# Up-projections of a ConvFFN trunk: nine of 22 chunks per layer by seven products, in pairs, with more low parts made by accumulating DMA

## The chip, the cores and the metric

The kernel runs on one core of a Trainium2 chip. TensorE (PE in the profile) multiplies matrices out of SBUF into the banks of PSUM; VectorE (DVE), ScalarE (ACT) and GpSimd (POOL) work on elements; SyncE (SP) only issues DMAs here. Each engine has a queue of its own and works through it in order; an instruction that needs another engine's result waits on a semaphore, and everything behind it on its queue waits too. The metric is the device time of one execution in microseconds (us), as the median of several runs. Lower is better.

## The reference

Two layers over a residual stream of 512 tokens by 1024 features, all in float32. Each layer has an attention and then a gated ConvFFN. Only the ConvFFN is touched here, and in it only the up-projection:

```python
def conv_ffn(xn, w_up, cw, cb, w_down):
    a = xn @ w_up                       # 512x1024 by 1024x5632
    ap = jnp.pad(a, ((0, 0), (CONV_W - 1, 0), (0, 0)))
    a = sum(ap[:, j:j + T] * cw[j] for j in range(CONV_W)) + cb    # three taps
    gate, val = jnp.split(a, 2, axis=-1)
    return (jax.nn.gelu(gate, approximate=True) * val) @ w_down
```

w_up has 5632 columns: 2816 gate columns and 2816 value columns. A chunk is 128 gate columns and the 128 value columns that go with them, so there are 22 chunks in a layer.

## The kernel before, in words

**Products in three parts.** TensorE multiplies in a shorter float format (float32r). To keep float32's accuracy each operand is split into a high part (the value cast down) and a low part (the value minus its high part), and each product is made of three: high by high, high by low and low by high (`mm3`, lines 260 to 263).

**Weights.** A piece is a tile of 128 x 1024 raw weights (512 KB): all 1024 rows of the 128 gate columns of a chunk, or of its value columns. The class `Weights` walks through all pieces of the kernel in one order. SP loads them (line 46), two pieces ahead of the split. `high()` casts a piece on ScalarE (line 54). The low part is made in one of two ways:

```python
    def low(self):            # VectorE: raw - high                          (line 66)
        self.nc.vector.tensor_tensor(pair[:, 1], raw, pair[:, 0].bitcast(F32), ALU.subtract)
    def high_added(self):     # ScalarE: pair[:, 1] = -raw, rounded (line 61); then a DMA adds raw (line 81)
        self.high(True)
        self.low_added()      # self.nc.gpsimd.dma_start(pair[:, 1], raw, accum_op=ALU.add)
```

The second way costs VectorE nothing: ScalarE writes a negated, rounded copy, and a DMA that is issued on GpSimd's queue reads the raw piece and adds it to that copy in SBUF. The raw tile can't be used again until that DMA has landed.

**Plain chunk.** Two pieces (gate, value), each in a bank of 128 x 512 of PSUM: 8 blocks of 128 rows of w_up, three products each, 512 tokens wide. That makes 48 matmuls of 512 columns (`up`).

**Seven-product chunk.** The chunk's product is written as a 2 x 2 block product: the weights as a11, a12 (the gate piece's first and second half of the rows of w_up) and a21, a22 (the value piece's), and the activations as four quarters (half of the features by half of the tokens, LO and HI). Strassen's scheme in Winograd's form then needs seven block products and not eight: with the weights A11, A12 and A22 and the sums S1 = a21 + a22, S2 = S1 - a11, S3 = a11 - a21, S4 = a12 - S2. Each block product is 4 blocks of rows by three parts, 12 matmuls of 256 columns, so a chunk has 84 of those (`prod`, `half_mm`). The four quarters of the result, o1 to o4, lie in the halves of two banks. Between the products o1 is copied out as s1 (ScalarE), and VectorE makes s12 = o2 + s1 and s17 = o3 + s1 (lines 926 and 927) and later adds them into o4, o3 and o2 (lines 935 to 941). A12 goes on in o1's place. The sums of the activations (XA, XB) are made once a layer by `sums_in`: two additions on GpSimd (line 646), then VectorE and ScalarE. The weights' sums and splits of a chunk are made by `seven_weights` (lines 665 to 694), a generator that is advanced piece by piece with `next(steps)`: two casts of 1024 for A11|A12 and S3|S2, one for S1|S4, one of 512 for A22, and the low parts all on VectorE (lines 683 to 690).

**Loop of a layer** (`ffn`, from line 602). Chunks 0 and 1 are made before the loop (`first_products`), and the weights of chunks 2 and 3 are split ahead (`W.split`). The loop then goes over c = 2 to 21. While TensorE works on chunk c, the other engines finish chunk c - 1 and prepare chunk c + 2:

- `product()`: VectorE multiplies gate by value of chunk c - 2 into hc (line 629), and GpSimd's queue stores the hc of the chunk before to memory (line 627);
- `taps()`: for the gate and the value bank of chunk c - 1 ScalarE makes the first tap and the bias (line 611), VectorE the other two taps (lines 612 and 614);
- `glu()`: ScalarE's GELU (line 632);
- `weights(c + 2)`: the steps that prepare the weights of chunk c + 2.

Seven-product chunks are 6, 8, ... 18 (seven in a layer), each with a plain chunk behind it. The four first row blocks of that plain chunk's first piece are multiplied inside the seven-product chunk, between A22 and S4 (`begun`), so that TensorE has work while S4 waits. Low parts by DMA are used for chunks 20 and 21 alone (four pieces a layer, `plain_weights`).

From chunk 18 on the layer's down-projection is prepared too: `pair_load` and `down_sums` load and add its weights, `pair_sums` (lines 725 to 728), `pair_highs` (line 735) and `pair_lows` (line 739) split the gated activations, which come back from memory.

**What sets the order.** The kernel runs under `manual_schedule`: each engine's queue holds its instructions in the order in which the program issues them. Tiles come from pools: p8 (16 tiles of two 1024-wide parts: split weights, activations' sums), p4 (10 tiles of 128 x 1024: raw weights, the weights' sums `wsum`, the taps' `bb`), p2 (8 small ones: hc, s1, s12, s17) and 8 banks of PSUM. An instruction that writes a new tile waits until the last reader of the tile's former content is done, and a DMA that reads it is such a reader.

Of the kernel before, what the change touches and what calls it, by code (L numbers as in the profile page):

```python
# [1 line left out]

# [6 lines left out]
F32 = mybir.dt.float32  # L9
F32R = mybir.dt.float32r  # L10
# [5 lines left out]
T = 512  # L16
# [10 lines left out]
SEVEN = range(6, 19, 2)  # L27
# [73 lines left out]
def trunk_kernel(ctx, tc, x, norm_gains, w_qkv_a, w_o_a, w_q_b, w_o_b, kv_norm, w_kvf, b_f,  # L101
# [500 lines left out]
    def ffn(l, bd, cp, nxt, ahead):  # L602
# [58 lines left out]
        halves = {}  # L661
# [6 lines left out]
        def seven_weights(c):  # L668

            r0, r1 = W.take(2)  # L670
            w = [t8([128, 2, 1024], F32R, name="w") for _ in range(4)]
            sa, sb = (t4([128, 1024], name="wsum") for _ in range(2))
            a11, a12, a21, a22 = r0[:, 0:512], r0[:, 512:1024], r1[:, 0:512], r1[:, 512:1024]
            act.copy(w[0][:, 0], r0)
            dve.tensor_tensor(sa[:, 0:512], a11, a21, ALU.subtract)
# [3 lines left out]
            act.copy(w[1][:, 0], sa)  # L679
            dve.tensor_tensor(sb[:, 512:1024], a12, sa[:, 512:1024], ALU.subtract)  # L680
            yield
            dve.tensor_tensor(w[1][:, 1], sa, w[1][:, 0].bitcast(F32), ALU.subtract)
            act.copy(w[2][:, 0], sb)
            yield
            dve.tensor_tensor(w[0][:, 1], r0, w[0][:, 0].bitcast(F32), ALU.subtract)
            act.copy(w[3][:, 0, 0:512], a22)
            yield
            dve.tensor_tensor(w[2][:, 1], sb, w[2][:, 0].bitcast(F32), ALU.subtract)
            yield
            dve.tensor_tensor(w[3][:, 1, 0:512], a22, w[3][:, 0, 0:512].bitcast(F32), ALU.subtract)  # L690
            v = [t.rearrange("p s (q k c) -> p s q k c", q=2, k=4) for t in w]
            halves[c] = dict(A11=v[0][:, :, 0], A12=v[0][:, :, 1], S3=v[1][:, :, 0], S2=v[1][:, :, 1],
                             S1=v[2][:, :, 0], S4=v[2][:, :, 1], A22=v[3][:, :, 0])

        def plain_weights(c):
            for _ in range(2):
                if c < NF - 2:
                    W.high()
                    W.low()
                else:  # L700
                    W.high_added()
                yield

        def weights(c):
            return seven_weights(c) if c in SEVEN else plain_weights(c)

# [191 lines left out]
        extra = sums_in()  # L898
        begun = None
        before = None  # L900
        for c in range(2, NF):
# [5 lines left out]
            steps = weights(c + 2) if c + 2 < NF else iter(())  # L907
            banks = [bank([128, T], name="up") for _ in range(2)]
            if c in SEVEN:
                w = halves.pop(c)  # L910
                W.n_get += 2
                x11, x21, x22 = [(xT[0][i], xT[1][i], s) for i, s in ((0, LO), (1, LO), (1, HI))]
                o1, o2, o3, o4 = banks[0][:, LO], banks[0][:, HI], banks[1][:, LO], banks[1][:, HI]
                s1, s12, s17 = (t2([128, 256], name="csum") for _ in range(3))

                def prod(o, a, x, start=False):
                    half_mm(o, w[a], x[0:2], x[2], start)

                prod(o1, "A11", x11, True)
                prod(o2, "S2", (*XB, HI))  # L920
                prod(o3, "S3", (*XA, HI), True)
                product()
                bb = taps(*before)
                act.copy(s1, o1)
                next(steps)
                dve.tensor_tensor(s12, o2, s1, ALU.add)
                dve.tensor_tensor(s17, o3, s1, ALU.add)
                glu(before[0], bb)
                prod(o1, "A12", x21)
                prod(o2, "S1", (*XA, LO))  # L930
                prod(o3, "A22", (*XB, LO))
                next(steps)
                next(steps, None)
                dve.tensor_tensor(o4, o2, s17, ALU.add)
                begun = W.get(), bank([128, T], name="up")
                up(*begun, range(4))
                prod(o2, "S4", x22)
# [756 lines left out]
```

## Time and profile before

| quantity | value |
|---|---|
| time, median of 3 runs | 1120.49 us (1119.68 to 1120.97) |
| time of the profiled execution | 1119.51 us |
| its span in the profile | 1117.5 us |
| TensorE's granted clock, mean | 0.999 of full speed |
| busy: TensorE | 1108.2 us, 99% |
| busy: VectorE | 891.2 us, 80% |
| busy: ScalarE | 614.0 us, 55% |
| busy: GpSimd | 182.8 us, 16% |
| moved by DMA | 217.34 MB, 194 GB/s in the mean |
| first up-projection of the loop (c = 2), layer 0 | starts at about 204.5 us of the span |
| first product of the down-projection, layer 0 | at about 417 us |

The span runs from the first to the last instruction; the profiled execution's own time is 2.0 us longer. Busy time is the time in which an engine executes, as a share of the span. A row of a view of single instructions gives the start (us from the start of the span), the length, the engine, the line of the source, the operation, output and inputs by the program's names, and the tiles' shapes; the brackets behind it say how long the engine was idle ahead of it and what ended that. Instructions of one engine overlap at their ends, so the distance from one start to the next is the price of an instruction in a full queue, and the length is not.

### The profile page before, as it was taken

Reading aid. Unit: us, or ns where it says so; the run is one execution under the profiler, and the core shown is the slowest. Engines: PE = TensorE matmul, PEld = TensorE weight load, DVE = VectorE, ACT = ScalarE, POOL = GpSimd, SP = SyncE. Lnnn points to the kernel's source line nnn. Section 1 sums busy time; section 2 is a strip of 40 time slices with the busy share of each in tenths; the row PEclk is TensorE's granted clock in tenths of the full one; section 3 lists DMA queues with packets and bytes.
Section 4 is the critical chain, followed back from the end, with each engine's and each line's share of the span. In section 5 each row is a group of like instructions: output and inputs, shape, how many; then the busy total and the mean of one; then the engine's idle time right before and its main releaser. Section 6 shows DMA issues by size and latency. Waiting matters only on the chain. (4 is left out here: it accounts for less than half of the span.)

```text
span 1117.5 us, 17262 instructions
## 1 busy us (share of the span) xinstructions
PE 1108.2 (99%) x6258; PEld 950.8 (85%) x6258; DVE 891.2 (80%) x1456; ACT 614.0 (55%) x1036; POOL 182.8 (16%) x277
## 2 busy tenths in 40 slices
PE   9999999999999999999999999999999999999997
PEld 6988889889899888888878888889889889988886
DVE  6567788888888689997697777848888888589894
ACT  5454575545445456576462688745445445457572
POOL 2832101200000121000001545500300000121000
PEclk9999999999999999999999999999999999999999
DMA  9469854343433699893447666464333444599862
GB/s 325 151 222 408 313 174 134 94 123 105 141 119 116 158 354 368 303 324 110 132 152 272 199 171 164 115 197 130 97 102 116 132 124 122 149 352 374 317 245 75
DMA packets 179183, 217.34 MB, mean 194 GB/s; under 512 B 11225, under 2 KB 131017, under 8 KB 179098
## 3 DMA queue, kind: packets, MB, share of 16 engines
q1 hardware_dynamic: 169594, 183.99, 50.6%
q0 software_dynamic: 9504, 32.25, 9.0%
q8 instruction: 49, 0.80, 0.3%
q14 instruction: 36, 0.29, 0.1%
HBM read 166.08 MB, written 39.63 MB: 184 GB/s over the span
## 5 line engine op out<-in xcount | busy, mean ns | idle before, releaser
L611 ACT ACTIVATE bb<-up,conv 128x512 f32<-128x512 f32 x80 | 60.7, 777 | 149.4 <-DVE up L941 76.2
L66 DVE TENSOR_TENSOR w<-wraw,w 128x1024 fp32r<-128x1024 f32 x98 | 125.0, 1306 | 18.4 <-ACT w L54 14.0
L261 PE MATMUL acc<-w 128*128 128x512 f32 (+1 forms) x311 | 120.6, 388 | 0.3 <-DVE mix L323 0.3
L263 PE MATMUL acc<-w 128*128 128x512 f32 (+1 forms) x311 | 120.4, 387 | 0.0
L54 ACT CAST w<-wraw 128x1024 fp32r<-128x1024 f32 x110 | 111.4, 1046 | 15.0 <-PE v_ps L262 6.9
L261 PE MATMUL up<-xch,w 128*128 128x512 f32 (+1 forms) x292 | 104.9, 359 | 0.0
L261 PE MATMUL up<-xbh,w 128*128 128x512 f32 (+1 forms) x292 | 104.8, 359 | 0.0
L262 PE MATMUL up<-xcl,w 128*128 128x512 f32 (+1 forms) x292 | 104.8, 359 | 0.0
L262 PE MATMUL up<-xbl,w 128*128 128x512 f32 (+1 forms) x292 | 104.8, 359 | 0.0
L263 PE MATMUL up<-xch,w 128*128 128x512 f32 (+1 forms) x292 | 104.7, 358 | 0.0
L263 PE MATMUL up<-xbh,w 128*128 128x512 f32 (+1 forms) x292 | 104.7, 358 | 0.0
L262 PE MATMUL acc<-w 128*128 128x512 f32 (+1 forms) x267 | 103.3, 387 | 0.0
L627 POOL DMA_DIRECT2D hD<-hc x42 | 24.3, 579 | 316.9 <-DVE hc L629 316.5
L261 PEld LDWEIGHTS acc<-w 128*128 128x128 f32 x311 | 58.4, 188 | 12.4 <-DVE mix L323 0.7
L263 PEld LDWEIGHTS acc<-w 128*128 128x128 f32 x311 | 58.4, 188 | 12.0 <-DVE w L739 0.2
L612 DVE SCALAR_TENSOR_TENSOR bb<-up,conv,bb 128x511 f32<-128x511 f32 x80 | 59.5, 744 | 7.8 <-ACT bb L611 7.8
L261 PE MATMUL up<-xsh,w 128*128 128x256 f32 x224 | 63.4, 283 | 0.0
L262 PE MATMUL up<-xsl,w 128*128 128x256 f32 x224 | 63.4, 283 | 0.0
L263 PE MATMUL up<-xsh,w 128*128 128x256 f32 x224 | 63.4, 283 | 0.0
L261 PEld LDWEIGHTS up<-xch,w 128*128 128x128 f32 x292 | 55.1, 189 | 8.3
L614 DVE SCALAR_TENSOR_TENSOR bb<-up,conv,bb 128x510 f32<-128x510 f32 x80 | 59.9, 749 | 2.8
L261 PEld LDWEIGHTS up<-xbh,w 128*128 128x128 f32 x292 | 55.1, 189 | 8.3
(310 smaller groups left out, 3018.1 us busy)
## 6 DMA issues: line engine op xcount, KB each, us to landing
wraw<-in_w_up_dram SPq DMA_DIRECT2D x88, 512.0 KB
dT<-dsums SPq DMA_DIRECT2D x24, 512.0 KB
dsums<-in_w_down_dram SPq DMA_DIRECT2D x22, 512.0 KB
dsums<-in_w_down_dram SPq DMA_DIRECT2D x44, 256.0 KB
hD<-hc POOLq DMA_DIRECT2D x44, 256.0 KB, 4.8
dact<-hD SPq DMA_DIRECT2D x44, 256.0 KB
wraw<-dT SPq DMA_DIRECT2D x22, 512.0 KB
wraw<-in_w_down_dram SPq DMA_DIRECT2D x22, 512.0 KB
```

Source lines behind the costliest of these rows:

```text
L54: self.nc.scalar.copy(pair[:, 0], raw)
L66: self.nc.vector.tensor_tensor(pair[:, 1], raw, pair[:, 0].bitcast(F32), ALU.subtract)
L261: pe.matmul(o, ah, bh, start=first, stop=False, skip_group_check=shared)
L262: pe.matmul(o, ah, bl, start=False, stop=False, skip_group_check=shared)
L263: pe.matmul(o, al, bh, start=False, stop=last, skip_group_check=shared)
L611: act.activation(bb[:, s, :], ps, AF.Identity, bias=cp[:, 3, ch:ch + 1], scale=cp[:, 2, ch:ch + 1])
L612: dve.scalar_tensor_tensor(bb[:, s, 1:], ps[:, :T - 1], cp[:, 1, ch:ch + 1], bb[:, s, 1:], ALU.mult, ALU.add)
L614: dve.scalar_tensor_tensor(bb[:, s, 2:], ps[:, :T - 2], cp[:, 0, ch:ch + 1], bb[:, s, 2:], ALU.mult, ALU.add)
L627: pool.dma_start(hD[c - 1], hc.pop(c - 1))
```

## The change

**More seven-product chunks, in pairs.** SEVEN becomes 6, 8, 9, 11, 12, 14, 15, 17, 18: nine a layer. Chunk 6 stands alone; then come four pairs of neighbours, with a plain chunk behind each pair.

**Low parts.** A table ADDED says which pieces of plain chunks get their low part by an accumulating DMA: the first pieces of chunks 4, 5, 7, 10, 13, 16 and 20 and the second pieces of 4, 5, 20 and 21. The others are subtracted by VectorE: so are both pieces of chunk 19 and, new, the first piece of chunk 21. In the first chunk of each pair, and in chunk 6 (chunks whose predecessor is plain), the three 1024-wide low parts (A11|A12, S3|S2, S1|S4) are made by DMA as well (`add_low`); in the second chunk of a pair VectorE subtracts them (`sub_low`), that of S1|S4 at a later place (`late`). The low part of A22 stays on VectorE throughout. That makes 26 accumulating DMAs a layer, where there were 4.

**Weights in two generators.** `weights_a(c)` runs during chunk c - 2 (A11|A12 and the first sums, or a plain chunk's two pieces), `weights_b(c)` during chunk c - 1 (S1|S4 and A22). The steps that are left at the end of a chunk now stay for the next one, unless the next chunk is plain or the one after it has seven products.

**Order of products.** The first chunk of a pair, and chunk 6, starts with A11; then come `begin()` inside the taps (the copy s1, the product S3, the sum s17, the product S2) and `join()` (s12), then A22, A12 and S1. Before its S4 the first chunk of a pair multiplies A11 and S3 of the second chunk; the second chunk then starts with S2 (`begun`). The second chunk has, ahead of its S4, the first half of the plain chunk's first piece, as every seven-product chunk had before. A22 now stands ahead of A12 and S1.

```diff
-SEVEN = range(6, 19, 2)
+SEVEN = 6, 8, 9, 11, 12, 14, 15, 17, 18
+
+ADDED = (4, 5, 7, 10, 13, 16, 20), (4, 5, 20, 21)
...
+        def add_low(w, raw):
+            act.activation(w[:, 1], raw, AF.Copy, scale=-1.0)
+            pool.dma_start(w[:, 1], raw, accum_op=ALU.add)
+
+        def sub_low(w, raw, n=1024):
+            dve.tensor_tensor(w[:, 1, :n], raw, w[:, 0, :n].bitcast(F32), ALU.subtract)
+
+        def weights_a(c):
+            if c >= NF:
+                return
+            if c not in SEVEN:
+                for i in range(2):
+                    if c in ADDED[i]:
+                        W.high_added()
+                    else:
+                        W.high()
+                        W.low()
+                    yield
+                return
             r0, r1 = W.take(2)
...
             act.copy(w[0][:, 0], r0)
+            if c - 1 not in SEVEN:
+                add_low(w[0], r0)
             dve.tensor_tensor(sa[:, 0:512], a11, a21, ALU.subtract)
             dve.tensor_tensor(sb[:, 0:512], a21, a22, ALU.add)
             yield
             dve.tensor_tensor(sa[:, 512:1024], sb[:, 0:512], a11, ALU.subtract)
-            act.copy(w[1][:, 0], sa)
+            if c - 1 not in SEVEN:
+                act.copy(w[1][:, 0], sa)
+                add_low(w[1], sa)
...
+        def weights_b(c):
+            if c not in SEVEN:
+                return
+            (w0, w1), r0, a12, a22, sa, sb = rest.pop(c)
+            if c - 1 in SEVEN:
+                act.copy(w1[:, 0], sa)
+                sub_low(w0, r0)
...
             dve.tensor_tensor(sb[:, 512:1024], a12, sa[:, 512:1024], ALU.subtract)
+            act.copy(w[1][:, 0, 0:512], a22)
+            if c - 1 in SEVEN:
+                sub_low(w1, sa)
             yield
+            act.copy(w[0][:, 0], sb)
+            if c - 1 in SEVEN:
+                late.append(lambda: sub_low(w[0], sb))
+            else:
+                add_low(w[0], sb)
+            sub_low(w[1], a22, 512)
...
-            steps = weights(c + 2) if c + 2 < NF else iter(())
+            steps = chain(steps, weights_b(c + 1), weights_a(c + 2))
...
+                def begin():
+                    act.copy(s1, o1)
+                    prod(o3, "S3", (*XA, HI), True)
+                    dve.tensor_tensor(s17, o3, s1, ALU.add)
+                    prod(o2, "S2", (*XB, HI))
+
+                def join():
+                    dve.tensor_tensor(s12, o2, s1, ALU.add)
+
+                if begun:
+                    prod(o2, "S2", (*XB, HI))
+                    product()
+                    join()
+                    bb = taps(*before)
+                else:
+                    prod(o1, "A11", x11, True)
+                    product()
+                    bb = taps(*before, begin)
+                    join()
+                prod(o3, "A22", (*XB, LO))
                 prod(o1, "A12", x21)
                 prod(o2, "S1", (*XA, LO))
...
                 dve.tensor_tensor(o4, o2, s17, ALU.add)
+                if c + 1 in SEVEN:
+                    begun = ([bank([128, T], name="up") for _ in range(2)],
+                             *(t2([128, 256], name="csum") for _ in range(2)))
+                    b1, b3 = (o[:, LO] for o in begun[0])
+                    prod(b1, "A11", x11, True, halves[c + 1])
+                    act.copy(begun[1], b1)
+                    prod(b3, "S3", (*XA, HI), True, halves[c + 1])
+                else:
+                    begun = W.get(), bank([128, T], name="up")
+                    up(*begun, range(4))
                 prod(o2, "S4", x22)
...
                 dve.tensor_tensor(o3, o3, s12, ALU.add)
+                if c + 1 in SEVEN:
+                    late.pop()()
+                    dve.tensor_tensor(begun[2], b3, begun[1], ALU.add)
...
                     if s == 0 and before:
-                        post(*before, (lambda: pair_lows(0)) if c == NF - 1 else None)
+                        product()
+                        bb = taps(*before, (lambda: pair_lows(0)) if c == NF - 1 else None)
+                        next(steps, None)
+                        glu(before[0], bb)
...
-            run(steps)
+            if c + 1 not in SEVEN or c + 2 in SEVEN:
+                run(steps)
```

More of the change, by code (lines that the diff above doesn't have):

```diff
@@ L1 @@
 from contextlib import ExitStack
+from itertools import chain
 import concourse.bass as bass
@@ L659, in sums_in @@
                     yield
-        halves = {}
+        halves, rest, late = {}, {}, []
         def split_pair(pair, src, n=1024):
@@ L688, in seven_weights @@
[L688 to L702, printed above, removed]
@@ L898, in ffn @@
         extra = sums_in()
+        steps = iter(())
         begun = None
@@ L916, in prod @@
-                def prod(o, a, x, start=False):
+                def prod(o, a, x, start=False, w=w):
                     half_mm(o, w[a], x[0:2], x[2], start)
[L919 to L927, printed above, removed]
```

44 lines of the change are left out of this document (25 added, 19 removed).

## The prediction

> **What bounds the kernel now.** I read the page first (busy times, and the chain that ended last), then the busy times of one stretch of the up-projections, then TensorE's instructions in it.
>
> ```profile
> span 1117.5 us, 17262 instructions
> ...
> PE 1108.2 (99%) x6258; PEld 950.8 (85%) x6258; DVE 891.2 (80%) x1456; ACT 614.0 (55%) x1036; POOL 182.8 (16%) x277
> ...
> PE 39%; DVE 1%; ACT 1%; issue 1%; DMA 0%; DVEq 0%; ACTq 0%
> ```
>
> TensorE is busy for 1108.2 of 1117.5 us, and of the engines the chain holds hardly anything but PE (39%; the next are DVE and ACT with 1% each). A busy PE can hide a slow PE, so the next view takes one seven-product chunk (c = 8) and the plain one behind it, from 248.2 to 269.2 us of the span. Its columns are the stretch, its length, busy time and count of each engine, granted clock, DMA share and GB/s.
>
> ```profile
> core 0: us, PE busy (x) PEld busy (x) DVE busy (x) ACT busy (x) POOL busy (x), PEclk, DMA share, GB/s
> 248.20:269.20 21.00, 21.00 (x134) 19.09 (x132) 16.98 (x25) 9.79 (x13) 0.54 (x1) 1.00 0.41 126
> ```
>
> PE has no hole, at the full clock (1.00). VectorE works 16.98 of 21.00 us (81%), ScalarE 9.79 (47%), GpSimd almost nothing, and the DMA engines 41%. TensorE's own instructions in it, start and length in us:
>
> ```profile
> 248.20 0.28 PE L261 MATMUL up<-xbh,w 128*128 128x256 f32 x1
> ...
> 256.83 0.40 PE L261 MATMUL up<-xbh,w 128*128 128x512 f32 x1
> ...
> 259.58 0.28 PE L261 MATMUL up<-xbh,w 128*128 128x256 f32 x1
> ...
> 261.01 0.40 PE L261 MATMUL up<-xbh,w 128*128 128x512 f32 x1
> ...
> 269.20 0.28 PE L261 MATMUL up<-xbh,w 128*128 128x256 f32 x1
> ```
>
> The lengths overlap, so only the starts count. From 248.20 to 256.83 come 72 products of 256 columns (8.63 us, 0.120 each) and from 259.58 to 261.01 the last 12 (1.43): 10.06 us for a seven-product chunk. From 256.83 to 259.58 (2.75) and from 261.01 to 269.20 (8.19) come the 48 products of 512 columns of the plain chunk: 10.94 us. Nothing waits here, so a chunk costs what its products cost, and less time on TensorE is less time of the kernel, as long as its operands arrive.
>
> **The gain.** The list of seven-product chunks grows from 7 (6, 8, ... 18) to 9 (6, 8, 9, 11, 12, 14, 15, 17, 18) in each of two layers: four chunks more, at 10.94 - 10.06 = 0.88 us, together 3.5 us. TensorE cannot give more here, since it has no idle time to lose.
>
> **What it costs the other engines.** Three chunks (two seven, one plain) now take 2 x 10.06 + 10.94 = 31.06 us. VectorE's prices, in the steady stretch:
>
> ```profile
> 252.71 0.43 DVE L927 TENSOR_TENSOR csum<-up,csum 128x256 f32<-128x256 f32 x1 [0.43 <-PE up L263]
> 253.05 0.68 DVE L678 TENSOR_TENSOR wsum<-wsum,wraw 128x512 f32<-128x512 f32 x1
> 253.77 0.69 DVE L680 TENSOR_TENSOR wsum<-wraw,wsum 128x512 f32<-128x512 f32 x1
> ...
> 257.37 1.22 DVE L685 TENSOR_TENSOR w<-wraw,w 128x1024 fp32r<-128x1024 f32 x1
> 258.50 0.43 DVE L939 TENSOR_TENSOR up<-up,csum 128x256 f32<-128x256 f32 x1
> 258.84 1.22 DVE L688 TENSOR_TENSOR w<-wsum,w 128x1024 fp32r<-128x1024 f32 x1
> ...
> 261.55 0.68 DVE L690 TENSOR_TENSOR w<-wraw,w 128x512 fp32r<-128x512 f32 x1
> 262.15 0.69 DVE L629 TENSOR_TENSOR hc<-bb 128x512 f32<-128x512 f32 x1
> 262.75 0.74 DVE L612 SCALAR_TENSOR_TENSOR bb<-up,conv,bb 128x511 f32<-128x511 f32 x1
> 263.53 0.75 DVE L614 SCALAR_TENSOR_TENSOR bb<-up,conv,bb 128x510 f32<-128x510 f32 x1
> 264.20 0.74 DVE L612 SCALAR_TENSOR_TENSOR bb<-up,conv,bb 128x511 f32<-128x511 f32 x1
> 264.97 0.75 DVE L614 SCALAR_TENSOR_TENSOR bb<-up,conv,bb 128x510 f32<-128x510 f32 x1
> ```
>
> From start to start: 1.13 us for a low part of 1024 (257.37 to 258.50), 0.34 for an addition of 256 columns (258.50 to 258.84), 0.60 for 512 (261.55 to 262.15) or 0.72 where the second uses the first's result (253.05 to 253.77), 0.78 and 0.66 for the two taps. A chunk's product and taps are 0.60 + 2 x (0.78 + 0.66) = 3.5 us. The first chunk of a pair has all three 1024-wide low parts made by DMA: sums of weights 2.6, low part of A22 0.6, five additions 1.7, in all 4.9. The second keeps three low parts on VectorE: 4.9 + 3 x 1.13 = 8.3. The plain one has one low part, 1.13. With three times 3.5 that is 24.8 of 31.06 us, 80% where it was 81%. VectorE does not become the bound.
>
> ScalarE and GpSimd make the DMA's part: a negated copy (first row below, made so late in the layer today), then the accumulating DMA, which starts on GpSimd when the copy has ended. The last three rows are landing times after issue: four such DMAs, one at a time, in the attention of the second layer (640 to 720 us), and two pairs late in the first layer's up-projections (378 to 384, 390 to 396), each pair some 2 us apart.
>
> ```profile
> 251.54 1.05 ACT L674 CAST w<-wraw 128x1024 fp32r<-128x1024 f32 x1
> ```
> ```profile
> 380.90 1.06 ACT L61 ACTIVATE w<-wraw 128x1024 fp32r<-128x1024 f32 x1
> ```
> ```profile
> 382.26 0.86 POOL L81 DMA_DIRECT2D w<-wraw  x1 [1.25 <-ACT w L61]
> ```
> ```profile
> DMA to landing us min/median/max: 6.2/6.2/6.4
> ...
> DMA to landing us min/median/max: 8.2/8.9/9.5
> ...
> DMA to landing us min/median/max: 8.6/9.2/9.9
> ```
>
> A copy is 0.95 us from start to start. Per three chunks ScalarE has eight casts of 1024 (three, three, two), two of 512 (A22; half price) and four negated copies: 13 x 0.95 = 12.4. Convolution and gate are 2.1 a chunk (9.79 less five and a half casts and one csum copy, halved). That makes 12.4 + 6.3 + 0.6 = 19.3 of 31 us, 62%. GpSimd issues four DMAs at 0.87 more, on an idle queue; there are 22 more in a layer, and behind each stands the store of hc, which nobody reads before chunk 18. From the end of the copy (381.96) to the issue (382.26) pass 0.3 us. **What a landing takes** is the unknown: 6.2 to 9.9 us by these rows. I take 6.4. In the new order two adds of a pair are 4 us apart, not 2, and the DMA share is 0.41 rather than full, so the single ones are nearer. [...]
>
> **The walk, t = 0 at the first product of a pair's first chunk.** TensorE: A11, S3, S2, A22, A12, S1 at 1.44 each, to 8.64; A11 and S3 of the second chunk to 11.52; S4 to 12.96; S2, A22, A12, S1 to 18.72; half of the plain piece to 21.45; S4 to 22.89; the rest to 31.06. A waiting engine starts 0.19 us after the last product's slot (row 252.71: the slot ends at 252.52).
> - First chunk. S3 ends at 2.88, so s17 starts at 3.07; two taps follow at 3.41 and 4.19, s12 at 4.85, done at 5.28. A12 overwrites o1's bank at 5.76 and waits for s12: 0.4 us spare, the tightest place. VectorE must be free by 3.07.
> - Low parts of the second chunk: A11's 5.2 to 6.4, needed at 8.64; S3's 6.9 to 8.15, needed at 10.1; S1's 9.6 to 10.8, needed at 17.3. All in time.
> - The plain piece's first half: VectorE's last weight sum ends at 7.0, ScalarE casts it and the piece to 8.96, negates to 10.0, and the add is issued at 10.3; its low part is wanted at 18.72 + 0.46 = 19.2. It may take 8.85 us.
> - The next pair's adds. Second chunk: S4 ends at 12.96, o2 and product to 14.1, s12 at 14.6, taps to 17.8 (ScalarE: gate to 17.05, cast to 18.0, negated copy to 19.1, A11's add at 19.4, wanted 31.3); the plain piece's low part to 18.95, two weight sums to 20.15, o4 to 20.5, S3's sum to 21.2, cast and negated copy to 23.2, S3's add at 23.5, wanted 32.7. Plain chunk: S4 ends at 22.89, o2 and product to 24.0, taps from 24.4 to 27.25, S1's sum to 27.95, two copies to 30.0, S1's add at 30.3, wanted 38.5. Room: 11.9, 9.2 and 8.2 us.
> - The new wait is on VectorE. In the plain chunk the sum a21 + a22 for the next pair's second chunk goes into a buffer of the pool that S3's add still reads. VectorE comes to it at 29.05 (27.25 and three times 0.60); the add lands at 23.5 + 6.4 = 29.9. Queued behind it are the product, two taps and then s17 of the next pair. From landing to s12's end are 0.60 + 0.72 + 0.60 + 0.78 + 0.66 + 0.34 + 0.78 + 0.66 + 0.43 + 0.05 = 5.6 us, and A12 waits at 31.06 + 5.76 = 36.8. So it costs nothing up to a landing at 31.2, that is 7.7 us after issue; beyond that, as many microseconds as the landing is late. At the first pair the issue comes earlier (12.2 us after chunk 6 starts, 21.0 before chunk 8) and 8.9 us are allowed.
>
> The SP queue's loads of raw weights take buffers that are freed later (by an add's landing, and by VectorE's second half of the sums), but each is issued 10 us or more before its cast. I cost them at nothing; the cover is those 10 us.
>
> **Layer start.** The first add of chunk 4 now stands on GpSimd ahead of the two sums of x.
>
> ```profile
> 206.05 2.94 ACT L54 CAST w<-wraw 128x1024 fp32r<-128x1024 f32 x3
> ```
> ```profile
> 191.42 10.19 POOL L646 TENSOR_TENSOR xsum<-xbh,xbl 128x2048 f32<-128x2048 f32 x2 [52.42 <-DVE xbl L353]
> ```
> ```profile
> 192.08 5.04 DVE L66 TENSOR_TENSOR w<-wraw,w 128x1024 fp32r<-128x1024 f32 x1
> ```
>
> Today these sums run from 191.42 to 201.6. In the new order the add waits for the negated copy, which ends at 209.0 (the third cast's place and one copy more), is issued at 209.3, and the sums run from 209.9 to 220.1. VectorE's first subtraction of them then has to wait. The row at 192.08 shows what a VectorE subtraction beside such a sum costs: 5.04 us instead of 1.22, ending as the first sum ends. So I take 220.1, not 215.0, for its start. From there VectorE has 25 us of work (at the prices above) before s17 of chunk 6, and waits for ScalarE's copies between; I get 251.7 instead of 251.3 for s17 and 253.9 for s12's end, where A12 wants it at 254.0, an estimate good to half a microsecond. Cost 0, with nothing spare; at most one subtraction more, 1.2 us a layer. [...]
>
> **Layer end.** The low part of chunk 21's first piece goes back to VectorE, and chunk 18 starts with two products done.
>
> ```profile
> 395.42 0.68 DVE L629 TENSOR_TENSOR hc<-bb 128x512 f32<-128x512 f32 x1
> ...
> 403.23 0.69 DVE L580 TENSOR_TENSOR dsums<-dsums 128x512 f32<-128x512 f32 x1 [0.94 <-DMA dsums<-in_w_down_dram]
> ...
> 411.95 0.43 DVE L725 TENSOR_TENSOR dact<-dact 128x256 f32<-128x256 f32 x1 [1.14 <-DMA dact<-hD]
> ```
>
> VectorE reaches hc (395.42) 1.13 us later, loses 0.9 of it at the wait at 403.23 for a DMA, and the rest at 411.95 (1.14 us of waiting for a DMA). One add less is in flight there. I cost it at 0.1.
>
> **Sum.** -3.5 + 0.1 = -3.4 us: 1119.5 -> 1116.1 for the profiled execution, which lies 1.0 below the median 1120.49; on the median 1117.1.
>
> **The rivals.**
> - *B, slower: the adds land late.* With pairs of adds and three loads around them they land as in the crowded rows. At 8.9 us (the second row's middle) S3's add costs 8.9 - 7.7 = 1.2 us at three pairs and 0 at the first, in two layers, and the plain piece's 0.05 at three places in two: 7.5, so 1124.6. At 9.2 (the third row's) it is 1.5 x 6 + 0.3 x 2 + 0.35 x 6 = 11.7, so 1128.8. The gain is gone from a landing of 8.3 us on (0.6 x 6 = 3.6). For it: every one of these rows from up-projections is over 8. Against it: there the DMA share is full, here 0.41 plus the adds.
> - *C, part of it is lost:* s12 late at chunk 6 by up to 1.2 us a layer, or adds at 8.0 us (0.3 x 6): 1.8 to 2.4 us lost, 1118.9 to 1119.5. For it: no spare time in either place.
> - *D, nothing comes of it:* the layer's end is bound by DMA (share 1.02 from 387 to 417, below) and what comes earlier only waits there: 1120.5. Against it: its loads start on the same products as before, so they come earlier too.
>
> ```profile
> 387.00:417.00 30.00, 30.00 (x135) 24.83 (x134) 25.61 (x40) 16.49 (x20) 7.11 (x12) 1.00 1.02 339
> ```
>
> **The numbers.** Forecast (A) 60%, its own range 1116.2 to 1118.0; C 9%; D 4%; B 27%, 5 of it (landings of 8.3 to 8.6) within 0.2% of no change. The time is A's 1117.1. From 1116.0 (A less the runs' spread of 1.1 us) to 1123.0 leaves out most of B beyond a landing of 8.7, 2 in 10. A measurement can tell 0.2%, 2.2 us, from no change: faster is A, 60%; the same are C, D and B's start, 18%; slower the rest of B, 22%.
>
> **What would show it.** Right: TensorE's starts in a pair and its plain chunk repeat every 31.06 us; the adds land in 6 to 7.7 us; the sum behind the add starts by 30; A12 does not wait; GpSimd's sums at 210 to 220. Wrong: a hole in PE ahead of A12 with s12 (VectorE) as releaser, VectorE idle on GpSimd's add for over 2 us, landings over 8, or the raw weights late on the SP queue.

## The result, and the profile after

The changed kernel takes 1117.1 us (median of 8 runs, 1116.29 to 1118.08) against 1120.4 us (8 runs, 1119.48 to 1121.28): a ratio of 0.9972, 95% interval 0.9961 to 0.9982. The profiled execution went from 1119.51 to 1116.29 us. The page of the changed kernel:

```profile
span 1114.5 us, 17752 instructions
...
PE 1104.6 (99%) x6402; PEld 954.3 (86%) x6402; DVE 866.0 (78%) x1456; ACT 663.5 (60%) x1092; POOL 219.4 (20%) x321
...
w<-wraw POOLq DMA_DIRECT2D x36, 512.0 KB, 7.3
```

TensorE is as full as before and has less to do. VectorE lost 25 us, ScalarE gained 50 and GpSimd 37, all on engines with room. The last line is the adds (36 of them with a raw piece, in the whole kernel), with their median landing.

TensorE's starts in the changed kernel: a pair (from 300.18), its plain chunk's first piece, the next pair, the first piece behind chunk 18's last product, and the down-projection. Below them the last two in the kernel before.

```profile
300.18 0.28 PE L264 MATMUL up<-xbh,w 128*128 128x256 f32 x1
...
318.89 0.40 PE L264 MATMUL up<-xbh,w 128*128 128x512 f32 x1
...
331.26 0.28 PE L264 MATMUL up<-xbh,w 128*128 128x256 f32 x1
...
385.23 0.40 PE L264 MATMUL up<-xbh,w 128*128 128x512 f32 x1
...
415.18 0.39 PE L264 MATMUL acc<-w 128*128 128x512 f32 x1
```
```profile
387.01 0.40 PE L261 MATMUL up<-xbh,w 128*128 128x512 f32 x1
...
416.96 0.39 PE L261 MATMUL acc<-w 128*128 128x512 f32 x1
```

A pair with its plain chunk takes 331.26 - 300.18 = 31.08 us, and the down-projection begins 29.95 us after chunk 18 in both kernels (415.18 - 385.23 and 416.96 - 387.01). So the gain is made between chunk 6 and chunk 18 and kept. The busy times of that stretch, in the columns of the prediction's view, show no hole, and the DMA engines at 82%:

```profile
300.18:331.26 31.08, 31.08 (x217) 29.16 (x216) 24.93 (x40) 19.52 (x26) 5.12 (x9) 1.00 0.82 195
```

GpSimd's issues in the same stretch, in order: the plain piece's add, A11's, S3's and S1's. Then the landing times after issue, of all pairs' adds from 266 to 390 us, of the plain pieces' from 266 to 375, and of the add of chunk 7's first piece alone.

```profile
310.53 0.85 POOL L84 DMA_DIRECT2D w<-wraw  x1 [9.73 <-ACT w L64]
...
319.56 0.86 POOL L674 DMA_DIRECT2D w<-wraw  x1 [7.61 <-ACT w L673]
323.74 0.86 POOL L674 DMA_DIRECT2D w<-wsum  x1 [3.33 <-DVE up L999]
...
330.46 0.85 POOL L674 DMA_DIRECT2D w<-wsum  x1 [5.29 <-DVE wsum L701]
```
```profile
DMA to landing us min/median/max: 5.0/5.6/6.6
...
DMA to landing us min/median/max: 7.5/7.8/8.3
...
DMA to landing us min/median/max: 7.9/7.9/7.9
```

With t = 0 at 300.18 the four are issued at 10.35, 19.38, 23.56 and 30.28 us, where the walk had 10.3, 19.4, 23.5 and 30.3. VectorE at the new wait, and around chunk 6:

```profile
214.95 5.63 DVE L651 TENSOR_TENSOR xsum<-xsum 128x1024 f32<-128x1024 f32 x1 [6.71 <-POOL xsum L649]
...
251.24 0.42 DVE L955 TENSOR_TENSOR csum<-up,csum 128x256 f32<-128x256 f32 x1 [0.34 <-PE up L266]
...
253.03 0.41 DVE L959 TENSOR_TENSOR csum<-up,csum 128x256 f32<-128x256 f32 x1
...
329.55 0.69 DVE L701 TENSOR_TENSOR wsum<-wraw 128x512 f32<-128x512 f32 x1 [0.22 <-DMA w<-wsum]
```

The sum behind S3's add waits 0.22 us for the landing and starts at t = 29.37. In chunk 6 VectorE waits for TensorE ahead of s17 (0.34 us), not the other way round, and s12 is done at 253.44, where A12 comes at 253.86 (248.10 and 5.76).

The time has one way to be lost: the operands. The experiments go after that.

### The profile page after: what moved, and what is told of

It is laid out like the page before. It is cut to its first block, busy times and chain, and to the rows that moved or that the text cites. A ratio compares the mean times of both kernels' runs of the same rounds, so it can differ in the third digit from the quotient of the medians.

```text
span 1114.5 us, 17752 instructions
## 1 busy us (share of the span) xinstructions
PE 1104.6 (99%) x6402; PEld 954.3 (86%) x6402; DVE 866.0 (78%) x1456; ACT 663.5 (60%) x1092; POOL 219.4 (20%) x321
## 4 chain that ended last, share of the span: by engine, by line
PE 94%; issue 2%; DVE 2%; POOL 1%; ACT 1%; DMA 0%; DVEq 0%; POOLq 0%
PE up L265 13%; PE up L264 13%; PE up L266 13%; PE acc L264 8%; PE acc L266 8%; PE acc L265 8%; PE qk_ps L265 2%; PE qk_ps L264 2%; PE qk_ps L266 2%; PE v_ps L264 2%; PE v_ps L266 2%; PE v_ps L265 2%; PE o_ps L1642 2%; PE s_ps L1594 1%; PE first L266 1%
## 5 line engine op out<-in xcount | busy, mean ns | idle before, releaser
L57 ACT CAST w<-wraw 128x1024 fp32r<-128x1024 f32 x102 | 104.8, 1048 | 15.7 <-PE v_ps L265 6.9
L69 DVE TENSOR_TENSOR w<-wraw,w 128x1024 fp32r<-128x1024 f32 x76 | 91.8, 1231 | 15.5 <-ACT w L57 15.0
L265 PE MATMUL up<-xbl,w 128*128 128x512 f32 (+1 forms) x284 | 99.2, 349 | 0.0
L265 PE MATMUL up<-xcl,w 128*128 128x512 f32 (+1 forms) x284 | 99.2, 349 | 0.0
L264 PE MATMUL up<-xbh,w 128*128 128x512 f32 (+1 forms) x284 | 99.1, 349 | 0.0
L264 PE MATMUL up<-xch,w 128*128 128x512 f32 (+1 forms) x284 | 99.1, 349 | 0.0
L266 PE MATMUL up<-xbh,w 128*128 128x512 f32 (+1 forms) x284 | 99.0, 349 | 0.0
L266 PE MATMUL up<-xch,w 128*128 128x512 f32 (+1 forms) x284 | 99.0, 349 | 0.0
L264 PE MATMUL up<-xsh,w 128*128 128x256 f32 x288 | 81.5, 283 | 0.0
L265 PE MATMUL up<-xsl,w 128*128 128x256 f32 x288 | 81.5, 283 | 0.0
L266 PE MATMUL up<-xsh,w 128*128 128x256 f32 x288 | 81.5, 283 | 0.0
L84 POOL DMA_DIRECT2D w<-wraw x26 | 24.7, 956 | 284.8 <-ACT w L64 248.4
```

The lines of the kernel that those rows point to most:

```text
L57: self.nc.scalar.copy(pair[:, 0], raw)
L264: pe.matmul(o, ah, bh, start=first, stop=False, skip_group_check=shared)
L265: pe.matmul(o, ah, bl, start=False, stop=False, skip_group_check=shared)
L266: pe.matmul(o, al, bh, start=False, stop=last, skip_group_check=shared)
```

## The experiments

All ratios are to the kernel before, whose median in these comparisons was 1120.07 to 1120.44 us.

**Is it the number of chunks?** First the old list of seven chunks in the new code, and a list of eight:

```diff
-SEVEN = 6, 8, 9, 11, 12, 14, 15, 17, 18
+SEVEN = 6, 8, 10, 12, 14, 16, 18                                        # seven_chunks
-ADDED = (4, 5, 7, 10, 13, 16, 20), (4, 5, 20, 21)
+ADDED = (4, 5, 7, 9, 11, 13, 15, 17, 20), (4, 5, 20, 21)
```
```diff
-SEVEN = 6, 8, 9, 11, 12, 14, 15, 17, 18
+SEVEN = 6, 8, 9, 11, 12, 14, 15, 17                                     # eight_chunks
```

> The changed kernel with the old list of seven chunks (6, 8, ... 18), each alone: all their 1024-wide low parts by accumulating DMA, and the first pieces of the plain chunks between them too (34 DMAs a layer), the new order of products kept. Theory (only the count of products on TensorE sets the time, and the 22 more DMAs and the lighter VectorE are worth nothing by themselves): the time of the kernel before, 1120.4 us, within 0.7, and TensorE's starts repeat every 21.0 us per pair of chunks. Rival 1 (part of the gain comes from the relief of VectorE, not from the two chunks more): 1 to 3 us under the kernel before. Rival 2 (the DMAs cost something that the gain covers): 1 us or more over it.

> The changed kernel with chunk 18 plain again: 6, 8, 9, 11, 12, 14, 15, 17, eight a layer. Theory: half of the gain, two chunks at 0.84 us less than the kernel before (and two more than the changed one): 1118.8 us, within 0.7. If the pairs as such cost or gain something, it is off that line: under 1118.0 or over 1119.5.

Eight gave 1118.67 us (0.9984, 0.9975 to 0.9993), half of the gain as expected. Seven gave 1135.22 us (1.0128, 1.0115 to 1.0142): 15 us over the kernel before, for the same products. Rival 2 is right there, and far beyond its 1 us. What TensorE waited for in it, the two adds issued 1.89 us apart in each period, and the landing times of the second of them (266 to 375 us):

```profile
PE up L266 <- DMA w<-wraw: 6.8, 11, 1.5
PE up L266 <- DMA w<-wsum: 2.6, 9, 0.5
```
```profile
292.20 0.86 POOL L674 DMA_DIRECT2D w<-wsum  x1 [8.42 <-ACT w L673]
294.09 0.86 POOL L84 DMA_DIRECT2D w<-wraw  x1 [1.04 <-ACT w L64]
```
```profile
DMA to landing us min/median/max: 9.1/9.4/10.1
```

This is the case of the prediction's rival B: adds land after 9 us, and TensorE waits for low parts, here at the plain piece and at S1. In eight_chunks it happened twice in the first layer: 0.65 us at S1 of chunk 17, which stands alone there and whose add landed after 8.8 us, and once at the place where the changed kernel has least to spare, the first piece of chunk 7:

```profile
257.00 0.40 PE L265 MATMUL up<-xbl,w 128*128 128x512 f32 x1
258.05 0.50 PE L266 MATMUL up<-xbh,w 128*128 128x512 f32 x1 [0.64 <-DMA w<-wraw]
```
```profile
DMA to landing us min/median/max: 9.0/9.0/9.0
```

The add was issued at 249.0 there as in the changed kernel (248.97), but landed after 9.0 instead of 7.9 us, and the next matmul started 1.05 us after the last and not 0.23. Up to there the two run the same code; in the second layer of eight_chunks the same add landed after 8.2 us, and nothing was lost. So a few tenths of a microsecond decide whether this place waits; whether it waits in other executions of the changed kernel no trace shows.

**What makes an add land late?** My first answer was two adds close together. So the first pieces of the plain chunks went back to VectorE, in the kernel with seven chunks and in the one with nine (`plain_dve`):

```diff
-ADDED = (4, 5, 7, 9, 11, 13, 15, 17, 20), (4, 5, 20, 21)
+ADDED = (4, 5, 20), (4, 5, 20, 21)
```

> Seven single chunks again, now with the first pieces of the plain chunks between them subtracted by VectorE (in the run with them added by DMA, two adds were issued 1.9 us apart in each 21 us, landed after 8.5 and 9.1 to 10.1 us, and TensorE lost 0.7 to 1.9 us at the plain piece and 0.3 to 0.6 at S1 in each period). Theory (that crowding of two adds is the whole loss, and the count of products the rest): the add of S1 lands in 5 to 6 us, TensorE repeats every 21.0 us, 1120.4 us within 0.7. Rival (21 adds a layer cost something wherever they stand): 1122 us or more.

> The changed kernel with nine chunks, and the first pieces of chunks 7, 10, 13 and 16 subtracted by VectorE; the adds of the pairs' first chunks and of chunks 4, 5, 20 and 21 stay. Theory: VectorE has 1.13 us more in 31.08 (84% instead of 81%) and room for it between s12 and o4; the plain piece's add, which today lands after 7.5 to 8.3 us where 8.2 to 8.85 are allowed, is no longer there; so no loss in any execution: 1116.8 us within 0.6, and a narrower spread than the changed kernel's 1.8 us. Rival (VectorE has no 1.13 us to spare ahead of s12 in chunk 6 or o4 in a pair): 1118 us or more.

plain_dve gave 1116.49 us (0.9966, 0.9953 to 0.9978; 1115.87 to 1117.41), which can't be told from the changed kernel's 0.9972; the nine chunks don't need the adds of their plain pieces. seven_plain_dve gave 1126.31 us (1.0059, 1.0046 to 1.0071). Half of the loss was gone, and the theory with it: S1's add, now alone, still landed after 8.5 to 9.5 us in the first layer and after 8.1 to 8.9 in the second. The view of the transfers by queue, for the 4.0 us behind one such issue (290.39 us; q0 carries the adds, q1 the loads of SP), and what held SP's loads up to that moment (266 to 390 us):

```profile
q1 hardware_dynamic: 2154, 1.09, 101.3%
...
w<-wsum POOLq DMA_DIRECT2D x1, 512.0 KB, 9.0
```
```profile
SPq L49 <- DVE w L69: 37.0, 5, 7.7
SPq L49 <- DVE wsum L720: 30.7, 6, 5.8
```

The same view of the changed kernel, for 4.0 us behind the issue of S1's add at 330.46:

```profile
q0 software_dynamic: 170, 0.63, 84.6%
q1 hardware_dynamic: 72, 0.03, 2.9%
...
w<-wsum POOLq DMA_DIRECT2D x1, 512.0 KB, 5.0
```

In the first, loads of raw weights (1.09 MB) filled all 16 engines for 4 us, and not one packet of the add moved; in the second they were out of the way, its first packet moved 1.42 us after the issue, and it landed after 5.0 us. The loads wait for buffers, which VectorE frees with its last reads of raw weights (L69, L720) and the adds with their landings (25.9 us in four waits for such landings, in the same stretch); and L720, the sum for S1, is also what S1's add comes from. So the same instruction lets the loads go and, two copies later, the add. Over the 324 adds of six executions (the changed kernel, seven_chunks, eight_chunks, ten_chunks, seven_plain_dve, plain_dve) I took, from the packets, the time that q1's packets took between an add's issue and its landing, divided by the 16 engines. The landing is 5.2 us and 0.82 us for each such microsecond (correlation 0.87): 71 adds with under 0.5 us of it landed after 4.5 to 6.4 us, 89 with over 3.5 us after 6.9 to 12.2. A part of that comes by itself, since an add that is under way for longer meets more loads; with q1's time in the first 4.5 us alone, which every add is under way, the correlation is 0.75. The next experiment makes the transfer itself, in the kernel of plain_dve, beside S1's add in the first chunk of each pair:

```diff
-                add_low(w[0], sb)
+                add_low(w[0], sb, c > 6)
...
+            if beside:
+                act.dma_start(spare, w_down[l][0:512, :])
```

> The kernel of plain_dve with a copy of 2 MB from memory to memory on ScalarE's queue (the loads' kind of queue, not GpSimd's) right behind the negated copy of S1's sum in the first chunk of each of the four pairs, so that it starts together with the add of S1. The copy does no work of the reference. That add lands after 5.0 to 5.6 us in plain_dve, and some 8.2 are allowed. In the runs so far (324 adds, from the packets of six runs) an add lands after 5.0 us and 0.85 us more for each microsecond that transfers of the other queues fill the DMA engines meanwhile. Theory (the adds are late where raw loads are in their way): a copy of 2 MB fills the engines for some 5 us, so the add lands after 8.5 to 10 us, TensorE waits at S1 for 0.3 to 1.8 us at each of the four pairs in two layers, and the time is 1119 to 1132 us. Rival (only transfers ahead of it on its own queue make an add late): landings stay at 5 to 6 us and the time at 1116.5 within 0.8.

The adds of S1 landed after 10.2 to 11.6 us, and the time was 1146.4 us (1.0242, 1.0208 to 1.0277). The same adds landed after 5.1 to 6.6 us in plain_dve. So a transfer on another queue does make an add late, as the theory had it. It is not the loads' case in every respect: by the list of packets the copy moves in packets of 64 KB and the loads in packets of 512 B, and no run holds back the loads themselves. TensorE's waits for such adds (in total, their count, the longest), the copy's queue in the whole kernel, the landing of the first add, the matmul that waited for it, and the busy times of two stretches behind:

```profile
PE up L266 <- DMA w<-wsum: 21.0, 8, 3.3
```
```profile
q10 hardware_dynamic: 384, 16.78, 4.6%
```
```profile
DMA to landing us min/median/max: 10.7/10.7/10.7
```
```profile
279.45 0.39 PE L266 MATMUL up<-xsh,w 128*128 128x256 f32 x1 [2.34 <-DMA w<-wsum]
```
```profile
280.01:283.42 3.41, 3.41 (x18) 3.41 (x17) 1.82 (x3) 0.00 (x0) 0.00 (x0) 0.50 1.20 309
283.40:287.40 4.00, 4.00 (x35) 4.00 (x34) 1.25 (x4) 0.54 (x2) 0.00 (x0) 1.00 0.65 157
```

The matmul started 2.62 us after the last one (276.83), 2.5 more than the usual 0.12: as late as the landing was beyond the 8.2 us allowed. The time was beyond my range for two reasons. The landings were later than the 8.5 to 10 us that I had expected (the 5 us for which the copy was to fill the engines were my estimate, and no run had shown them; its packets took 4.6% of the 16 engines' 1144.9 us, some 6.6 us for each of the eight copies), so that the eight waits alone cost 22.2 us (from start to start, beyond the usual 0.12). And behind five of them the clock was granted at 0.50 for 3.41 us (the first of the last two rows), 1.7 us each.

**What does a late landing cost at the new wait on VectorE?** A copy of 1 or 2 MB on GpSimd's own queue ahead of S3's add:

```diff
+            if behind:
+                pool.dma_start(spare, w_down[l][0:256, :])              # late_1mb; 0:512 in late_2mb
             pool.dma_start(w[:, 1], raw, accum_op=ALU.add)
...
-                add_low(w[1], sa)
+                add_low(w[1], sa, c > 6)
```

> The changed kernel with a copy of 1 MB from memory to memory on GpSimd's queue ahead of the add of S3 in the first chunk of each of the four pairs (not of chunk 6), to make that add land later. The copy does no work of the reference. Theory of the prediction: up to 7.7 us after its issue the landing costs nothing (8.9 at the first pair), then TensorE waits ahead of A12 as long as it is late. The add lands after 5.0 to 6.7 us today; I expect some 2.5 us more, 8 to 9 us: 0.3 to 1.3 us at three pairs in two layers, 1119 to 1126 us, with S1's add 7 us later late as well where the queue is still full. Rival (the wait on VectorE is taken in elsewhere): 1117.1, within 0.7.

> The same with a copy of 2 MB. I expect landings of 10 to 12 us: 2.3 to 4.3 us at three pairs in two layers and 1 to 3 at the first, 1133 to 1150 us. What matters is the step from the run with 1 MB: by the prediction's rule each microsecond of landing beyond 7.7 costs one microsecond at each pair.

1126.48 us (1.0056, 1.0042 to 1.0070) and 1146.29 us (1.0233, 1.0219 to 1.0247). In late_1mb the add issued at 293.67 landed after 9.1 us, and the one at 326.36 after 10.5; VectorE waited for the second, and TensorE behind the first, at A22 (the last product of S2 and the first of A22; L959 is the sum s17 in this kernel):

```profile
DMA to landing us min/median/max: 9.1/9.1/9.1
...
DMA to landing us min/median/max: 10.5/10.5/10.5
```
```profile
336.90 0.69 DVE L705 TENSOR_TENSOR wsum<-wraw 128x512 f32<-128x512 f32 x1 [4.95 <-DMA w<-wsum]
```
```profile
305.46 0.28 PE L266 MATMUL up<-xsh,w 128*128 128x256 f32 x1
306.68 0.39 PE L264 MATMUL up<-xsh,w 128*128 128x256 f32 x1 [0.94 <-DVE csum L959]
```

In late_2mb the first pair's landing was 9.4 us and the second's 11.4, and the period behind the second, by TensorE's starts:

```profile
DMA to landing us min/median/max: 9.4/9.4/9.4
...
DMA to landing us min/median/max: 11.4/11.4/11.4
```
```profile
302.49 0.28 PE L264 MATMUL up<-xbh,w 128*128 128x256 f32 x1
...
337.40 0.28 PE L264 MATMUL up<-xbh,w 128*128 128x256 f32 x1
```

By the prediction's rule (nothing up to 7.7, 8.9 at the first pair, then one for one) 9.1, 10.5, 9.4 and 11.4 us cost 1.4, 2.8, 0.5 and 3.7. Measured, as the period of TensorE's starts that follows, less 31.08: 1.61, 3.05, 0.48 and 3.83 (337.40 - 302.49 = 34.91). The rule holds within 0.3 us, in these four and at the other twelve pairs of the two runs (landings of 7.3 to 13.5 us; the layers' last pairs taken up to their last S4). Where TensorE waits isn't where the walk had it. In the first it waits at A22 (0.94 us) and loses only 0.2 us more at A12. In the second and the fourth it waits first at S3, whose low part this very add makes, and loses 1.4 and 2.2 us there: as much as the landing is beyond the 9.2 us of room that the prediction gave S3. In late_2mb a part of the loss is time at the halved clock (0.62 in the mean from 341.20 to 345.30 us).

**Are the adds needed at all?** All low parts of chunks up to 19 by VectorE:

```diff
-ADDED = (4, 5, 7, 10, 13, 16, 20), (4, 5, 20, 21)
+ADDED = (20,), (20, 21)
...
-            act.activation(w[:, 1], raw, AF.Copy, scale=-1.0)
-            pool.dma_start(w[:, 1], raw, accum_op=ALU.add)
+            sub_low(w, raw)
```

> The changed kernel with nine chunks in the same pairs, but all low parts subtracted by VectorE; only the three pieces of chunks 20 and 21 that were added stay with DMA. Theory (the low parts by DMA are what lets VectorE carry pairs): VectorE then has 4.5 us more in 31.08, 25.0 + 4.5 = 29.5 us, 95%, and most of it comes in the second chunk of a pair and the plain one, where its waits ahead of the next pair's s17 add up to some 1.7 us in the trace; s17 and s12 come late by 1 to 3 us at each pair, TensorE waits ahead of A12, and the time is 1122 to 1135 us. Rival (VectorE's waits take it all in, the DMAs are not needed): 1117.1, within 0.7.

1128.99 us (1.0076, 1.0062 to 1.0089), as the theory had it. TensorE's waits (in total, their count, the longest), and the busy times of 31 us:

```profile
PE up L264 <- DVE csum L954: 6.9, 6, 1.2
```
```profile
300.00:331.00 31.00, 29.62 (x208) 27.33 (x207) 27.98 (x41) 15.13 (x21) 1.63 (x3) 1.00 0.36 109
```

VectorE is busy for 28 of 31 us, and TensorE waits for s17 (L954 in this kernel) at A22, in the last three pairs of each layer. plain_dve did without the plain pieces' adds between the pairs, so the adds of the pairs' first chunks carry the change. The expectation for eleven, further down, takes these waits for s12; they are s17.

**Where does it stop?** Ten chunks to the layer's end, ten from chunk 5 (with and without the plain pieces' adds), and eleven:

```diff
+SEVEN = 6, 7, 9, 10, 12, 13, 15, 16, 18, 19                             # ten_chunks
+ADDED = (4, 5, 8, 11, 14, 17, 20), (4, 5, 20, 21)
...
+SEVEN = 5, 6, 8, 9, 11, 12, 14, 15, 17, 18                              # ten_from_5, ten_from_5_dve
+ADDED = (4, 7, 10, 13, 16, 20), (4, 20, 21)                             # ten_from_5; _dve: (4, 20), (4, 20, 21)
         extra = sums_in()
+        next(extra)
...
+SEVEN = 5, 6, 8, 9, 10, 12, 13, 14, 16, 17, 18                          # eleven, else as ten_from_5_dve
```

> Ten chunks a layer, all in pairs: 6, 7, 9, 10, 12, 13, 15, 16, 18, 19; first pieces of 4, 5, 8, 11, 14, 17, 20 and second ones of 4, 5, 20, 21 by DMA. If TensorE alone decides: two chunks more at 0.84, 1115.4 us. The theory expects the cover to run out in one of two places: at chunk 6 (VectorE has 0.34 us to spare there in the changed kernel, after 3.0 and 2.4 us of waiting for ScalarE ahead of it, and gets 0.7 us more to do), and at the layer's end, where VectorE is busy 29.0 of 30 us (387 to 417 us) and gets some 6 us more before it. Expected 1115.4 to 1119, with holes in TensorE after chunk 19.

> Ten chunks a layer in five pairs from chunk 5 on: 5, 6, 8, 9, 11, 12, 14, 15, 17, 18; so that the layer's end stays as in the changed kernel (with chunk 19 among the seven-product ones TensorE lost 1.8 us at chunk 20 and 4 at the down-projection, in each layer). For that GpSimd's two sums of x go first, before the adds of chunk 4; first pieces of 4, 7, 10, 13, 16, 20 and second ones of 4, 20, 21 by DMA. Theory: two chunks more at 0.84 us, 1115.4 us within 0.8, if VectorE makes chunk 5: between 204 and 240 us I count some 25 us of work for it (three chunks' taps, four sums and four low parts of x, the weights of 5 and part of 6) with waits for ScalarE between. If it doesn't, TensorE waits at chunk 5, and the time is 1116 to 1122 us.

> The same ten chunks with the first pieces of chunks 7, 10, 13 and 16 subtracted by VectorE, as in plain_dve (1116.5 us with nine). Theory: 1114.8 us within 0.8, and no wait for a plain piece's low part; the layer's start as in ten_from_5.

> Where the gain stops: eleven chunks a layer, a pair and three groups of three (5, 6; 8, 9, 10; 12, 13, 14; 16, 17, 18), else as ten_from_5_dve (1114.6 us). TensorE's count alone: two chunks less than that at 0.84 us, 1112.9 us. Theory (VectorE is the next bound): the third chunk of a group brings 8.3 + 3.5 = 11.8 us of VectorE's work in 10.06 us, and a group of three with its plain chunk 25.9 + 11.8 = 37.7 us in 41.1, 92%; at 95% (all_vectore) TensorE waited some 2.2 us for s12 and o4 in each period. I expect TensorE to wait for VectorE (s12, o4 or a low part) in the third chunk or at the start of the next group, 1 to 4 us at each of six groups: 1118 to 1137 us.

ten_chunks gave 1130.28 us (1.0085, 1.0071 to 1.0098), out of the range I gave it. The loss stands at the layer's end, one of the two places named (at chunk 6 it is 0.2 us), and its price was larger: behind the waits there the clock was granted at 0.50 as well, from 423.67 us for 6.83 us in the first layer. ten_from_5 gave 1114.71 us (0.9949, 0.9937 to 0.9962) and ten_from_5_dve 1114.56 (0.9950, 0.9936 to 0.9963): both lie 0.2% below the changed kernel's ratio, with intervals that touch. The traces show the difference: from chunk 2 to the down-projection the first layer takes 209.8 us in both, where the changed kernel takes 210.6, and TensorE waits for nothing in their up-projections. eleven gave 1125.15 us (1.0043, 1.0027 to 1.0060). TensorE's largest waits in ten_chunks, then in eleven:

```profile
PE acc L266 <- DVE w L767: 3.5, 2, 1.8
PE up L266 <- DMA w<-wraw: 2.9, 2, 1.5
PE acc L265 <- DVE w L767: 2.8, 2, 1.4
```
```profile
PE up L264 <- DVE up L980: 6.5, 6, 1.1
```

In ten_chunks the add of chunk 20's first piece landed after 10.4 us, and VectorE came late to the down-projection's low parts (L767). In eleven a group of three with its plain chunk takes 43.12 us where the products take 41.14 (31.08 and 10.06); it is lost where S4 must wait until VectorE has read its bank for o4 (L980): VectorE is the next bound.

## Why the prediction was right, and where its steps were not

- **The bound and the gain: right.** TensorE had no idle time, and took less when it had less to do. The size was 4 x 0.84 = 3.4 us and not 3.5: a pair's 13 block products take 18.71 us (318.89 - 300.18), 1.44 each, where I had 10.06 us for a chunk with two switches of size. 7 x 21.00 - (21.00 + 4 x 31.08) = 1.68 us a layer. The layer's end cost nothing instead of 0.1. The two errors cancel in the sum of -3.4, by luck. The profiled execution moved by 3.2 us; from the first layer's down-projection to the second's loop, code that isn't touched, it took 0.3 us longer.
- **VectorE and ScalarE: right.** 24.93 us against 24.8 forecast, and 19.52 against 19.3. The walk's times for the issues are right to 0.1 us.
- **The landing time: the value did, the reason didn't.** I took 6.4 us because two adds stand 4 us apart and the DMA share was 0.41. The share is 0.82, and the adds of S3 land after 5.0 to 6.7 us all the same; seven_plain_dve has single adds that land after 9. What goes with a late landing in the traces is the raw loads that stand ahead, and I had costed those at nothing, asking only whether the loads come in time and not what they do to an add. That they are mostly out of the way of the pairs' adds in the changed kernel was luck. Of the plain pieces' adds 6.4 was wrong by a microsecond and more: 7.5 to 8.3 us, with 8.85 allowed. So one of my signs of being wrong, landings over 8, did show, at places where it cost nothing.
- **The tightest place was another one.** I named A12 behind s12. Nothing waited there; the add of chunk 7's first piece (issued at 248.97, wanted some 8.2 us later) has 0.3 us to spare, and eight_chunks lost 0.8 us there. And where VectorE does come late (late_1mb, late_2mb, all_vectore) TensorE stands at A22, a wait that the walk doesn't have: A22 goes on in o3's bank, which s17 reads. By the walk s17 is done at 3.5 us and A22 starts at 4.32, 0.8 us of room against A12's 0.4, so A12 still sets the price, and the rule came out right.
- **The layer's start: right.** GpSimd's sums ran from 209.98 to 219.5 (forecast 209.9 to 220.1), and VectorE's subtraction took 5.63 us beside the second, instead of 1.22, as the prediction's row had it; it ended 1.1 us behind the sum (220.58 and 219.48). Chunk 6 had 0.3 us more to spare than I had worked out.
- **Rival B** didn't happen, but not for the reason I gave against it. Its price for S3's add was right (late_1mb, late_2mb), and its case, adds that land after 9 us in the middle of the up-projections, is seven_chunks, where they cost time at the plain piece and at S1 instead. **C and D** didn't happen either.

## What to carry to other kernels

An engine that is full gives back what its work is cut by only while every operand comes in time (one landing of 9.1 us cost 1.61 us in late_1mb), so a change to it is priced by the room of each transfer that it adds: issue, landing and first use, for each place of the period, the odd first one included. A landing time depends on what else is in the DMA engines at that moment (S1's add took 5.0 us with 0.03 MB of loads in the 4 us behind its issue in the changed kernel, and 9.0 us with 1.09 MB in seven_plain_dve): before taking one from another stage, look at which loads are set off by the buffers that are freed just ahead of it. And a DMA that takes work from a busy engine is worth it only there; the adds of the plain pieces bought nothing that could be measured (1117.1 us with them, 1116.49 without), and in a shorter period they cost 9 us (1135.22 and 1126.31).

## What the runs showed of the hardware

An accumulating DMA of 512 KB from GpSimd landed after 4.5 to 6.4 us where little else moved (the 71 adds with under 0.5 us of q1's time), and in two traces its first packets came behind the transfers of another queue rather than between them. In the changed kernel the first packet moved 1.42 us after the issue at 330.46, while q1 held 2.9% of the engines; in seven_plain_dve it took 4.06 us behind the issue at 290.39, while q1 held 101%. In beside_2mb, behind the issue at 303.90, the copy's second packets of 64 KB started from 3.0 us on, and the add's first packet only after 6.3 us. Why it moved so late no trace shows.

The clock fell behind short waits of TensorE: in beside_2mb to 0.50 behind five waits of 2.6 to 3.4 us (from start to start), and not behind others of 2.2, 3.2 and 3.5 us. By the trace's clock records each fall lasted 3.41 us, and the five began at 280.01, 348.28, 880.76, 918.30 and 952.43 us, whole multiples of 3.413 us apart (20, 156, 11 and 10, together 197 in 672.42 us). Where it fell, a wait was dearer by some 1.7 us (3.41 us at 0.50). In late_2mb a wait of 2.3 us was enough (338.95 to 341.23, the fall at 342.14). What decides behind which waits the clock falls, no run shows.
